# Four fast block pairs in each MLP unit, and low parts made by ScalarE and an adding DMA

## The chip, the cores and the metric

The kernel runs on one core of one Trainium2 chip. The metric is the device time of one execution in microseconds, given as the median of three runs.

## What is computed

Two layers of a decoder on one sequence of 256 rows of 2048. Each layer mixes two groups of attention heads and then runs an MLP; the part that matters here is the MLP, which is most of the arithmetic:

```python
hm = rms_norm(x, mlp_norm)
up = jnp.square(jax.nn.relu(jnp.einsum('bsd,df->bsf', hm, w_up)))      # 2048 -> 8192
return x + jnp.einsum('bsf,fd->bsd', up, w_down)                       # 8192 -> 2048
```

Everything is in float32 and every weight is read from HBM once.

## The kernel before

**Three matmuls for one.** A float32 product is made of matmuls on a shorter format. Each weight tile is split in a high part (`whi`, a rounding copy on ScalarE) and a low part (`wlo`, weight minus high part, on VectorE); activations are split alike. One block product is then three matmuls: high by high, high by low, low by high.

**Units and pairs.** The MLP of a layer is 16 units: four quarters `q` of the hidden width, each with two up units (`n2` = 0, 1) and two down units. I call them first up, second up, first down, second down, and the four together a quarter. A unit multiplies 256 rows by a 2048 x 1024 piece of the weights. It runs over eight *pairs*; a pair is two blocks of 128 contraction rows by 1024 columns, one load of 1 MB. A pair is a 2 x 2 by 2 x 2 block product. A plain pair takes eight block products, 24 matmuls of 128 x 512, in two steps of 12. A *fast* pair (`fast(i)`, pairs 1, 3 and 5) takes seven, 21 matmuls in four steps, for which VectorE first makes sums of the weight blocks in place and in the tiles `ts` (128x1024) and `t4` (`steps`, line 1208), and the activations get three extra blocks (`forms`, line 402).

**Banks and the end of a unit.** The sums of products lie in eight PSUM banks, 1 to 8. Plain steps add to banks 2 and 4, then 3 and 8; fast steps to 2 and 3, 4, 5 and 7, 1 and 6. At the end a tail on ScalarE and VectorE combines them (`down_tail`, `up_tail`): after the last fast pair a copy of bank 1, a difference with bank 6 and sums with 5 and 7; after the last plain steps one addition for each of banks 2, 4, 3 and 8. The next unit starts with banks 2 and 4, and may touch a bank only when the tail has read it. After an up unit TensorE also turns the squared result (transposes behind the first two steps of the next unit, line 1389).

**Who sets the order.** `Plan` (line 42) takes all pieces of a layer's MLP with lengths and dependences, lets TensorE and the load queue run in the order of writing, and on VectorE and ScalarE takes the ready piece that is due first. The result is a fixed order for each engine; at run time each engine works through its queue in order and stands still at a piece that isn't ready. Its lengths are

```python
        MM, TR, V2, V1, A2, A1 = 0.227, 0.108, 1.15, 0.61, 1.0, 0.55
        RING, RAWS = 5, 4
```

`RING` says that five tiles of high and five of low parts exist: a step's tile can be written when TensorE is through with the step five before. `RAWS` says the same of the loaded weights: a load waits until the pair four before has been read (`load`, line 1157; `parts`, line 1179).

**GpSimd** builds constants at the start (`build_constants`, line 238), clears a tile `kdz` in each layer and does some work in the attention; in the MLP it has nothing to do.

Of the kernel before, what the change touches and what calls it, by code (L numbers as in the profile page):

```python
# [17 lines left out]
P = 128  # L18
EPS = 1e-6
WARM0, WARM1 = 8, 6  # L20
DEPTH = 2
D = 2048
T = 256
# [16 lines left out]
class Plan:  # L40

# [26 lines left out]
    def run(self):  # L68
# [8 lines left out]
        line = {e: [p for p in self.pieces if p.engine == e] for e in ("PE", "SP")}  # L77
        free = dict.fromkeys(("PE", "SP", "DVE", "ACT"), 0.0)
# [48 lines left out]
def trunk_kernel(  # L127
# [60 lines left out]
    ATT = ("v4", "lr", "lrT", "ha", "hh", "hl", "hA", "on", "dec", "S", "kdz", "row", "bc")  # L188
    MLP = ("whi5", "wlo5", "sxh", "sx", "ts", "t4", "raw2")
# [36 lines left out]
    ident16 = cpool.tile([P, P], BF16, name="ident16")  # L226
    mask16 = cpool.tile([P, P], BF16, name="mask16")
    tri = cpool.tile([P, P], F32R, name="tri")
    nones = cpool.tile([P, P], F32R, name="nones")
    gmask = cpool.tile([P, CHUNK], F32, name="gmask")  # L230
    reset = cpool.tile([P, T], F32, name="reset")
    kdz = {}

# [4 lines left out]
    def build_constants():  # L238
        nc.vector.tensor_copy(ident16, ident)
# [8 lines left out]
        tri_f, nones_f = tmp("t2", [P, P], bufs=4), tmp("t2", [P, P], bufs=4)  # L248
# [32 lines left out]
    def load_gains(b, srcs):  # L281
        r = 0
        graw[b] = tmp("t2", [P, P], bufs=4)[: (NA, NB)[b]]
# [18 lines left out]
    wg = cpool.tile([RANK + 1, 512], F32, name="wg")  # L302

    def load_gate_up(l):
        nc.sync.dma_start(wg[0:RANK], w_gate_up[l])
        nc.sync.dma_start(wg[RANK : RANK + 1], b_gate[l : l + 1, :])
# [91 lines left out]
    def fast(i):  # L398
        return i in (1, 3, 5)

    def forms(op, i, t, tag):
# [6 lines left out]
        def sums():  # L408
            a11, a21, a12, a22 = (t[:, k, r * P : (r + 1) * P] for k in range(2) for r in range(2))
            e.append(tmp("e", [P, 3, P], bufs=2))  # L410
# [5 lines left out]
        def high():  # L416
            if e:
                op.x[i] = tmp(tag, [P, 3, 2, P], F32R, bufs=3)
                todo.append((op.x[i], e[0]))
# [10 lines left out]
    def operand_parts(op, n, h2, key, l, place):  # L430
# [30 lines left out]
        def scaled():  # L461
            t = tmp("t2", [P, 2, T], bufs=4)
# [17 lines left out]
    def norm_squares(n, ssq):  # L480
        for tt in range(NT):
            junk = tmp("t2", [P, 512], bufs=4)
# [124 lines left out]
    def join(acc):  # L607

        t = tmp("t2", [P, 2, T], bufs=4)
# [4 lines left out]
    def head_sums(ss, src, nh):  # L614

        sq = tmp("t2", [P, 512], bufs=4)
# [55 lines left out]
    def sb_scores(qT, kT, h):  # L672
# [11 lines left out]
        for j in range(2):  # L684
            for o in (zA[:, j * T : j * T + P], zB[:, j * P : (j + 1) * P]):
                nc.tensor.matmul(
                    o, ident16, mask16, start=False, stop=(j == 1), skip_group_check=True
# [16 lines left out]
    def sb_weights(za, zb, sph, spl):  # L704
        for part in (spl, sph):
            p0, p1 = part[:, : 2 * T], part[:, 2 * T :]
            upper = za.rearrange("p (h t) -> p h t", t=T)[:, :, P:T]
            for o, lhs, rhs in (
                (za, tri, p0), (zb, tri, p1),
                (upper, nones, p1.rearrange("p (h t) -> p h t", t=P)),  # L710
# [65 lines left out]
    for l in range(DEPTH):  # L776
# [290 lines left out]
        def pair_order(u):  # L1067

            if units[u][0] != "o":
                return range(8), {j for j in range(8) if fast(j)}  # L1070
# [544 lines left out]
```

## Time and profile before

| | us |
|---|---|
| median of three runs | 2185.19 (2185.18 to 2186.57) |
| the profiled execution | 2186.74 |
| its span, first to last instruction | 2185.0 |
| TensorE busy in it | 2176.2 |
| VectorE | 1850.9 |
| ScalarE | 1275.3 |
| GpSimd | 38.0 |

The span is shorter than the execution's own time by what lies around the first and the last instruction, 1.74 us. The profile's page has a table of engines, a chain of the work that ended last, and groups of instructions by line; the trace also answers with busy times by stretch and with single instructions in order of time. Matmul durations overlap there (each shows 0.39 us while the next starts 0.23 us later), so distances of starts are read, not durations.

### The profile page before, as it was taken

How to read it: one execution, taken by the hardware profiler on the slowest of the kernel's cores; microseconds unless marked ns; L12 is line 12 of the kernel's file. 1: busy time of each engine (PE TensorE's matmuls, PEld its weight loads, DVE VectorE, ACT ScalarE, POOL GpSimd, SP SyncE). 2: the span in 40 equal slices, each digit the busy share in tenths (PEclk: the TensorE clock that was granted, in tenths of full speed). 3: DMA queues.
4: the chain of work that ended last, by engine and by line, in shares of the span. 5: the costliest groups of instructions: out<-in, count | busy, mean ns of one | idle time of the engine just before them, and what ended most of it. 6: DMA issues, size and time to landing. Idle time of an engine off the chain costs nothing.

```text
span 2185.0 us, 27186 instructions
## 1 busy us (share of the span) xinstructions
PE 2176.2 (100%) x10352; PEld 1803.3 (83%) x10352; DVE 1850.9 (85%) x2386; ACT 1275.3 (58%) x1651; POOL 38.0 (2%) x64
## 2 busy tenths in 40 slices
PE   9999999999999999999999999999999999999999
PEld 7988778888888888888888887788888888888887
DVE  5677569999999999999957775799999999999998
ACT  5555356665566566466555553666665655665663
POOL 0020000000000000000000200000000000000000
PEclk9999999999999999999999999999999999999999
DMA  6654455466556556656556544555656565565564
GB/s 225 196 162 154 154 174 193 156 211 211 188 198 204 184 200 202 212 187 198 174 157 193 172 157 153 174 174 193 213 173 211 198 207 193 193 212 184 201 199 148
DMA packets 144359, 408.98 MB, mean 187 GB/s; under 512 B 6650, under 2 KB 31810, under 8 KB 144228
## 3 DMA queue, kind: packets, MB, share of 16 engines
q1 hardware_dynamic: 144228, 407.24, 56.7%
q8 instruction: 81, 1.33, 0.2%
q14 instruction: 50, 0.41, 0.1%
HBM read 405.12 MB, written 2.10 MB: 186 GB/s over the span
## 4 chain that ended last, share of the span: by engine, by line
PE 98%; DVE 1%; issue 0%; ACT 0%; DMA 0%; POOL 0%; SPq 0%; ACTq 0%
PE acc L549 6%; PE acc L551 6%; PE acc L550 6%; PE acc L596 3%; PE acc L600 1%; PE ps L1017 1%; PE ps L1029 1%; PE ps L976 0%; PE ps L712 0%; PE ps L658 0%; PE ps L676 0%; DVE wlo L1195 0%; PE ps L441 0%; PE ps L993 0%; PE ps L876 0%
## 5 line engine op out<-in xcount | busy, mean ns | idle before, releaser
L1191 ACT ACTIVATE whi<-raw 128x1024 fp32r<-128x1024 f32 x592 | 616.3, 1057 | 347.9 <-ACT whi L1191 11.5
L1195 DVE TENSOR_TENSOR wlo<-raw,whi 128x1024 fp32r<-128x1024 f32 x592 | 716.8, 1220 | 90.6 <-ACT whi L1191 85.6
L532 DVE TENSOR_TENSOR wlo<-raw,whi 128x1024 fp32r<-128x1024 f32 (+2 forms) x194 | 220.5, 1140 | 133.2 <-ACT whi L530 133.0
L530 ACT ACTIVATE whi<-raw 128x1024 fp32r<-128x1024 f32 (+2 forms) x194 | 189.7, 983 | 205.9 <-PE acc L551 156.3
L549 PE MATMUL acc<-whi,act 128*128 128x512 f32 (+2 forms) x640 | 243.1, 380 | 0.5 <-ACT act L451 0.5
L550 PE MATMUL acc<-wlo,act 128*128 128x512 f32 (+2 forms) x640 | 237.9, 372 | 0.0
L551 PE MATMUL acc<-whi,act 128*128 128x512 f32 (+2 forms) x640 | 237.5, 371 | 0.0
L1191 ACT ACTIVATE whi<-t 128x512 fp32r<-128x512 f32 x104 | 65.6, 631 | 162.8 <-DVE t L1058 154.8
L549 PEld LDWEIGHTS acc<-whi,act 128*128 128x128 f32 x640 | 121.2, 189 | 23.6 <-issue 4.1
L551 PEld LDWEIGHTS acc<-whi,act 128*128 128x128 f32 x640 | 120.9, 189 | 21.4 <-issue 0.7
L550 PEld LDWEIGHTS acc<-wlo,act 128*128 128x128 f32 x640 | 121.1, 189 | 19.1 <-issue 0.7
L1195 DVE TENSOR_TENSOR wlo<-ts,whi 128x1024 fp32r<-128x1024 f32 x104 | 127.2, 1223 | 7.3 <-ACT whi L1191 6.4
L1191 ACT ACTIVATE whi<-ts 128x1024 fp32r<-128x1024 f32 x104 | 109.6, 1054 | 35.1 <-PE m__2427_11949 L1284 2.1
L1058 DVE TENSOR_TENSOR ts<-raw 128x1024 f32<-128x1024 f32 x104 | 127.0, 1221 | 1.3
L596 PE MATMUL acc<-act,whi 128*128 128x512 f32 x256 | 91.9, 402 | 0.0
L1195 DVE TENSOR_TENSOR wlo<-t,whi 128x512 fp32r<-128x512 f32 x104 | 71.2, 685 | 2.8 <-ACT whi L1191 2.8
L600 PE MATMUL acc<-act,wlo 128*128 128x256 f32 x256 | 71.8, 280 | 0.0
L1058 DVE TENSOR_TENSOR raw<-ts,raw 128x512 f32<-128x512 f32 x104 | 71.2, 684 | 0.1
L1058 DVE TENSOR_TENSOR t<-raw 128x512 f32<-128x512 f32 x104 | 71.2, 684 | 0.1
L1368 ACT ACTIVATE act<-act,st 128x512 f32<-128x512 f32 x64 | 44.3, 717 | 26.5 <-DVE act L1058 26.5
L596 PEld LDWEIGHTS acc<-act,whi 128*128 128x128 f32 x256 | 48.1, 188 | 11.1
L600 PEld LDWEIGHTS acc<-act,wlo 128*128 128x128 f32 x256 | 48.4, 189 | 0.1
(2748 smaller groups left out, 5163.2 us busy)
## 6 DMA issues: line engine op xcount, KB each, us to landing
raw<-in_w_up_dram SPq DMA_DIRECT2D x128, 1024.0 KB, 5.1
raw<-in_w_down_dram SPq DMA_DIRECT2D x128, 1024.0 KB, 5.2
raw<-in_w_in_dram SPq DMA_DIRECT2D x84, 1024.0 KB, 5.2
raw<-in_w_o_dram SPq DMA_DIRECT2D x32, 1024.0 KB, 5.2
raw<-in_w_in_dram SPq DMA_DIRECT2D x14, 512.0 KB, 6.6
raw<-in_w_in_dram SPq DMA_DIRECT2D x8, 544.0 KB, 3.8
out_dram<-xb SPq DMA_DIRECT2D x8, 256.0 KB, 3.4
xb<-in_x_dram SPq DMA_DIRECT2D x3, 512.0 KB, 8.0
```

What stands on the lines that cost most here:

```text
L530: newest["hi"] = nc.scalar.activation(h, r, AF.Copy).ins
L532: newest["lo"] = nc.vector.tensor_tensor(lo[:, q : q + step, :width], r, f32(h), ALU.subtract).ins
L549: nc.tensor.matmul(o, xh[:, sl], whi[:, j, :width], start=first, stop=False)
L550: nc.tensor.matmul(o, xh[:, sl], wlo[:, j, :width], start=False, stop=False)
L551: st["mm"] = nc.tensor.matmul(o, xl[:, sl], whi[:, j, :width], start=False, stop=last).ins
L596: nc.tensor.matmul(acc[:, f, :], whi[:, j, sl], op.both(k), start=(k == 0), stop=False, skip_group_check=True,)
L600: nc.tensor.matmul(acc[:, f, T:], wlo[:, j, sl], xh, start=False, stop=(k == KT - 1), skip_group_check=True,)
L1017: nc.tensor.matmul(o, sc[:, (2 * tt + j) * P : (2 * tt + j + 1) * P], v[:, tt, vc + j * P : vc + (j + 1) * P], start=first, stop=False, sk ...
L1058: nc.vector.tensor_tensor(dst, a, b, op)
L1191: nc.scalar.activation(box["h"][:, :n], src(), AF.Copy)
L1195: nc.vector.tensor_tensor(box["l"][:, :n], src(), f32(box["h"][:, :n]), ALU.subtract)
L1368: nc.scalar.activation(box[h][:, tt, :], box[h][:, tt, :], AF.Relu, scale=rr[:, tt : tt + 1],)
```

## The change

In the MLP's up and down units pair 6 becomes fast as well (four of eight). Pairs 2 and 7 stay plain, but their low parts are no longer made by VectorE: ScalarE writes the negated high part into a tile `dlo` (two exist), and a DMA queued on GpSimd adds the weights to it. The steps stand in a new order, in which the steps of pairs 2 and 3 alternate, and a fast pair's steps run 2 and 3; 5 and 7; 1 and 6; 4. The low tiles of VectorE become four; the sum that went to `t4` is written in place. To make room, constants of the attention move into tiles that live only through the attention and are built again for layer 1, attention outputs `on` get two tiles for four, and the sums of the activations share the tiles `t2` (five for four).

```diff
+STEPS = [0, 0, 1, 1, 1, 1, 2, 3, 3, 2, 3, 3, 4, 4, 5, 5, 5, 5, 6, 6, 6, 6, 7, 7]
+FAST = (1, 3, 5, 6)
+ADDED = (2, 7)
...
-        RING, RAWS = 5, 4
+        RING, LOWS, ADDS, RAWS = 5, 4, 2, 4
...
+            return STEPS, FAST
+
+        def step_banks(kind, is_fast):
+
+            if kind == "g":
+                return (1, 6), (1, 6)
+            return ((2, 3), (5, 7), (1, 6), (4,)) if is_fast else ((2, 4), (3, 8))
...
+            def negated():
+                box["l"] = tmp("dlo", [P, 2, 512], F32R, bufs=ADDS)
+                nc.scalar.activation(box["l"], src(), AF.Copy, scale=-1.0)
+
+            def add_weights():
+                nc.gpsimd.dma_start(f32(box["l"]), src(), accum_op=ALU.add)
+
+            if by_dma:
+                m = add("ACT", A2, negated, deps, dlo[-ADDS] if len(dlo) >= ADDS else [])
+                lo = add("POOL", 2.7, add_weights, m, lag=7.0)
+                dlo.append([])
+                readers.extend((m, lo))
+            h = add("ACT", A2 if n == 2 else A1, high, deps, whi[-RING], last.get("h"))
+            whi.append([])
+            if not by_dma:
+                lo = add("DVE", V2 if n == 2 else V1, low, h, wlo[-LOWS], last.get("l"))
...
+                        by_dma=kind in ("up", "down") and j in ADDED,
...
-            t4 = add("DVE", V1, fourth, t2, sums4[-1] if sums4 else [])
+            t4 = vector(w(1, 0), w(0, 1), w(1, 0), t2, low[1:3])
...
+                if kind != "g" and k == max(last_use[m] for m in (5, 7, 1, 6)):
                     tails[u][0](p)
+                for c, ms in enumerate(((2, 4), (3, 8))):
+                    if kind != "g" and k == max(last_use[m] for m in ms):
+                        tails[u][1](c, p)
...
             load_gate_up(l)
+            after(2, build_constants)
```

The steps of a unit after the change are numbered 0 to 23, as `STEPS` lists them: 18 to 21 are pair 6, 22 and 23 pair 7.

VectorE's queue at the end of a first down unit (layer 0, first quarter), before the change. `xb` are the output tiles, `m1__` to `m8__` the banks, `t2` the tail's scratch; `wlo` are low parts, of the unit's last pair and then of the next unit's first pair (`raw2_934`); `ts_958` is the sum for the next unit's pair 1.

```order
L1195 TENSOR_TENSOR wlo_951_4767<-raw_926_4649,whi_946_4746 128x1024
L1058 TENSOR_TENSOR xb0_101<-m1__912_4583,xb0_101 128x512
L1058 TENSOR_TENSOR xb1_102<-t2_949_4756,xb1_102 128x512
L1195 TENSOR_TENSOR wlo_954_4787<-raw2_934_4680,whi_950_4764 128x1024
L1058 TENSOR_TENSOR t2_949_4756<-m7__908_4573,t2_949_4756 128x512
L1195 TENSOR_TENSOR wlo5_955_4796<-raw2_934_4680,whi5_953_4784 128x1024
L1058 TENSOR_TENSOR xb0_101<-xb0_101,t2_949_4756 128x512
L1058 TENSOR_TENSOR xb0_101<-m2__883_4469,xb0_101 128x512
L1058 TENSOR_TENSOR ts_958_4816<-raw_940_4716 128x1024
L1058 TENSOR_TENSOR xb0_101<-m4__886_4482,xb0_101 128x512
```

The same place after the change. The two low parts of the next unit are `wlo_966` and `wlo_969`.

```order
L1066 TENSOR_TENSOR xb0_94<-m1__916_4594,xb0_94 128x512
L1213 TENSOR_TENSOR wlo_966_4828<-raw2_943_4717,whi5_964_4819 128x1024
L1066 TENSOR_TENSOR t2_965_4826<-m6__919_4602,t2_965_4826 128x512
L1213 TENSOR_TENSOR wlo_969_4844<-raw2_943_4717,whi_967_4833 128x1024
L1066 TENSOR_TENSOR xb1_95<-t2_965_4826,xb1_95 128x512
L1066 TENSOR_TENSOR xb0_94<-m2__890_4484,xb0_94 128x512
L1066 TENSOR_TENSOR t2_965_4826<-m7__915_4589,t2_965_4826 128x512
L1066 TENSOR_TENSOR ts_971_4863<-raw_953_4767 128x1024
L1066 TENSOR_TENSOR xb0_94<-xb0_94,t2_965_4826 128x512
L1066 TENSOR_TENSOR xb1_95<-m3__898_4524,xb1_95 128x512
L1066 TENSOR_TENSOR xb0_94<-m4__893_4497,xb0_94 128x512
```

The addition that frees bank 4 now has two low parts, a sum and seven tail operations ahead of it, counted from the one that reads bank 1; between the last fast step and the next unit TensorE now has 27 matmuls where it had 48.

VectorE's queue at the end of a second up unit before the change (layer 0, first quarter; `act` holds the up unit's result, `wlo` are low parts of the next unit's first pair).

```order
L1058 TENSOR_TENSOR t2_872_4396<-m6__832_4214,act_868_4383 128x512
L1195 TENSOR_TENSOR wlo_873_4404<-raw2_851_4310,whi_871_4394 128x1024
L1058 TENSOR_TENSOR act_868_4383<-m7__826_4198,t2_872_4396 128x512
L1058 TENSOR_TENSOR act_869_4384<-m5__824_4188,t2_872_4396 128x512
L1058 TENSOR_TENSOR act_869_4384<-m5__824_4188,act_868_4383 128x512
L1195 TENSOR_TENSOR wlo_876_4425<-raw2_851_4310,whi_875_4414 128x1024
L1058 TENSOR_TENSOR ts_878_4435<-raw_859_4344 128x1024
L1058 TENSOR_TENSOR act_868_4383<-m2__800_4089,act_868_4383 128x512
```

The same place after the change.

```order
L1213 TENSOR_TENSOR wlo_882_4436<-raw2_857_4325,whi_879_4428 128x1024
L1066 TENSOR_TENSOR t2_884_4449<-m6__835_4215,act_880_4433 128x512
L1213 TENSOR_TENSOR wlo_886_4453<-raw2_857_4325,whi_883_4441 128x1024
L1066 TENSOR_TENSOR act_880_4433<-m7__830_4200,t2_884_4449 128x512
L1066 TENSOR_TENSOR act_881_4434<-m5__828_4190,t2_884_4449 128x512
L1066 TENSOR_TENSOR act_881_4434<-m5__828_4190,act_880_4433 128x512
L1066 TENSOR_TENSOR ts_888_4472<-raw_868_4377 128x1024
L1066 TENSOR_TENSOR act_880_4433<-m2__806_4097,act_880_4433 128x512
```

The order is nearly the same, with the low parts a place or two earlier against the tail; the sum for the next pair 1 stands ahead of the addition from bank 2 in both.

ScalarE's queue in the first down unit before the change: high parts of pair 5's last two steps and of the plain pairs 6 and 7.

```order
L1191 ACTIVATE whi_935_4688<-ts_923_4630 128x1024
L1191 ACTIVATE whi_938_4706<-raw_897_4528 128x1024
L1191 ACTIVATE whi5_941_4721<-raw_915_4595 128x1024
L1191 ACTIVATE whi_943_4731<-raw_915_4595 128x1024
L1191 ACTIVATE whi_944_4736<-raw_926_4649 128x1024
L1191 ACTIVATE whi_946_4746<-raw_926_4649 128x1024
```

The same place after the change: high parts of steps 16 and 17, then the two negated copies for steps 22 and 23, then the high parts of steps 18 to 20.

```order
L1209 ACTIVATE whi_942_4714<-raw_914_4587 128x1024
L1209 ACTIVATE whi_946_4736<-raw_914_4587 128x512
L1219 ACTIVATE dlo_948_4746<-raw_937_4687 128x1024
L1219 ACTIVATE dlo_949_4748<-raw_937_4687 128x1024
L1209 ACTIVATE whi_951_4759<-raw_927_4640 128x1024
L1209 ACTIVATE whi5_954_4769<-ts_950_4751 128x1024
L1209 ACTIVATE whi_956_4780<-raw_927_4640 128x1024
```

The two `dlo` copies are new there, and a copy that waits holds up the high parts behind it.

## Rows read from the trace of the kernel before

**Rows 1.** The page's span, and its table of engines: busy us, share, instructions.

```profile
span 2185.0 us, 27186 instructions
PE 2176.2 (100%) x10352; PEld 1803.3 (83%) x10352; DVE 1850.9 (85%) x2386; ACT 1275.3 (58%) x1651; POOL 38.0 (2%) x64
```

**Rows 2.** The page's chain of work that ended last, by engine.

```profile
PE 98%; DVE 1%; issue 0%; ACT 0%; DMA 0%; POOL 0%; SPq 0%; ACTq 0%
```

**Rows 3.** Busy times by stretch; one quarter of layer 0's MLP.

```profile
core 0: us, PE busy (x) PEld busy (x) DVE busy (x) ACT busy (x) POOL busy (x), PEclk, DMA share, GB/s
630.99:800.53 169.54, 169.54 (x765) 140.70 (x764) 157.55 (x188) 101.96 (x119) 0.00 (x0) 1.00 0.60 199
```

**Rows 4.** Timeline (start, us, engine, line): one matmul and its like one pairing later.

```profile
637.57 0.39 PE L1282 MATMUL m__1122_5588<-whi,act 128*128 128x512 f32 x1
...
647.77 0.39 PE L1282 MATMUL m__1122_5588<-whi,act 128*128 128x512 f32 x1
```

**Rows 5.** Timeline of VectorE in a second up unit.

```profile
635.29 0.29 DVE L411 TENSOR_TENSOR e<-act 128x128 f32<-128x128 f32 x1
635.61 0.29 DVE L412 TENSOR_TENSOR act<-act 128x128 f32<-128x128 f32 x1
...
640.52 0.55 DVE L426 TENSOR_TENSOR sx<-e,sx 128x384 fp32r<-128x384 f32 x1
...
647.81 1.22 DVE L1195 TENSOR_TENSOR wlo<-raw,whi 128x1024 fp32r<-128x1024 f32 x1
648.95 0.69 DVE L1058 TENSOR_TENSOR raw<-ts,raw 128x512 f32<-128x512 f32 x1
649.55 1.22 DVE L1195 TENSOR_TENSOR wlo<-raw,whi 128x1024 fp32r<-128x1024 f32 x1
```

**Rows 6.** Timeline of ScalarE in the same unit, a 128x512 high part.

```profile
641.17 0.62 ACT L1191 ACTIVATE whi<-t 128x512 fp32r<-128x512 f32 x1
```

**Rows 7.** Timeline at the end of layer 0's first down unit, TensorE and VectorE.

```profile
533.52 0.39 PE L1284 MATMUL m__912_4583<-whi,act 128*128 128x512 f32 x1
...
543.33 0.69 DVE L1058 TENSOR_TENSOR xb<-m__886_4482,xb 128x512 f32<-128x512 f32 x1
...
545.30 0.39 PE L1282 MATMUL m__959_4834<-whi,act 128*128 128x512 f32 x1
...
546.66 0.39 PE L1282 MATMUL m__960_4843<-whi,act 128*128 128x512 f32 x1
```

**Rows 8.** Timeline and chain: three hand-overs, TensorE to ScalarE, to VectorE, to TensorE.

```profile
642.78 0.39 PE L1284 MATMUL m__1101_5502<-whi,act 128*128 128x512 f32 x1
643.21 1.06 ACT L1191 ACTIVATE whi<-raw 128x1024 fp32r<-128x1024 f32 x1 [0.46 <-PE m__1101_5502 L1284]
...
656.18 1.06 ACT L1191 ACTIVATE whi<-raw 128x1024 fp32r<-128x1024 f32 x1 [1.65 <-PE m__1111_5540 L1284]
657.27 1.23 DVE L1195 TENSOR_TENSOR wlo<-raw,whi 128x1024 fp32r<-128x1024 f32 x1 [1.48 <-ACT whi L1191]
...
437.69 0.04 issue
437.74 0.50 PE m__715_3698 L1283
```

**Rows 9.** DMA issues: queue, count, KB each, median us to landing.

```profile
raw<-in_w_up_dram SPq DMA_DIRECT2D x128, 1024.0 KB, 5.1
out_dram<-xb SPq DMA_DIRECT2D x8, 256.0 KB, 3.4
```

**Rows 10.** Timeline of GpSimd and VectorE in layer 0's attention.

```profile
131.67 6.10 POOL L910 TENSOR_TENSOR act<-act,row 128x512 f32<-128x512 f32 x3
...
132.59 1.79 DVE L532 TENSOR_TENSOR wlo<-raw,whi 128x1024 fp32r<-128x1024 f32 x1 [0.45 <-ACT whi L530]
...
137.68 1.23 DVE L532 TENSOR_TENSOR wlo<-raw,whi 128x1024 fp32r<-128x1024 f32 x1 [1.07 <-ACT whi L530]
```

**Rows 11.** Groups of GpSimd's instructions by line: count, busy, mean ns.

```profile
L236 POOL MEMSET kdz<- 128x1536 f32 x2 | 2.8, 1382 | 811.9 <-DVE wlo L1195 811.9
```

More of the change, by code (lines that the diff above doesn't have):

```diff
@@ L246, in build_constants @@
         )
-        tri_f, nones_f = tmp("t2", [P, P], bufs=4), tmp("t2", [P, P], bufs=4)
+        tri_f, nones_f = (tmp("t2", [P, 512], bufs=T2)[:, :P] for _ in range(2))
         nc.gpsimd.memset(tri_f, -1.0)
@@ L1084, in trunk_kernel @@
             whi.append([p])
-            wlo.append([p])
+        wlo.extend([p] for p in before[-LOWS:])
         gate_done = {}
@@ new lines, in trunk_kernel @@
+            of_pair, uses = {j: 0 for j in order}, []
+            for j in order:
+                uses.append(step_banks(kind, j in quick)[of_pair[j]])
+                of_pair[j] += 1
+            last_use = {m: k for k, ms in enumerate(uses) for m in ms}
+            begun, p, running = set(), {}, {}
+            was = units[u - 1] if u else None
+            for k, j in enumerate(order):
+                if j not in running:
+                    running[j] = steps(u, j, j in quick, *load(u, j))
+                (box, h, lo, users), prods = next(running[j])
+                ready = done.get((kind, q, j))
+                for m, blocks in prods:
+                    begin, end = m not in begun, last_use[m] == k
+                    begun.add(m)
+                    p[m] = add(
+                        "PE", 3 * MM * len(blocks),
+                        lambda a=(m, blocks, box, begin, end): product(*a),
+                        h, lo, ready, free[m] if begin else [],
+                    )
+                    for tile_users in users:
+                        tile_users.append(p[m])
+                if kind == "g" and k == 4 or kind == "o" and n2 == 0 and k == 5:
+                    turn_gated()
+                    turn_gated()
+                if k < 2 and was and was[0] == "up":
+                    tails[u - 1][2](k)
+                if k < 2 and was and was[0] == "o":
+                    n = 2 * was[2] + k
+                    for h2 in range(2):
+                        done["up", 0, 2 * n + h2] = turned(
+                            n, h2, ((5, 7), (1, 6))[k][h2], hm, "mlp", l, sums=True
+                        )
+                if u + 1 == len(units) and k < 2 and l + 1 < DEPTH:
+                    for h2 in range(2):
+                        turned(k, h2, ((5, 7), (1, 6))[k][h2], hT, "attn", l + 1)
+                if kind != "g" and k == max(last_use[m] for m in (5, 7, 1, 6)):
```

193 lines of the change are left out of this document (77 added, 116 removed).

## The prediction

> **What bounds the kernel now.** First the page's table of engines: TensorE is busy 2176.2 of the 2185.0 us span [rows 1]. Then the chain that ended last: 98% of it is TensorE [rows 2]. So the end moves only if TensorE gets less to do, or is made to wait. The table of stretches, cut at one point of the repeating quarter of the MLP (two up units, two down units), gives 169.54 us a quarter, with VectorE busy 157.55, ScalarE 101.96, the DMA engines a 0.60 share [rows 3]. VectorE has 12 us to spare, so it is the next bound. Slots come from the timeline: 45 matmuls lie between the two rows of [rows 4], so one takes (647.77 - 637.57)/45 = 0.2267 us. On VectorE the distance of starts counts, not the duration shown: a 128x1024 operation holds the engine 1.14 us and shows 1.22, a 128x512 one 0.60 and shows 0.69 [rows 5].
>
> **What is removed.** One more pair by seven products saves three matmuls a unit, 32 units: 96 x 0.2267 = 21.8 us, all on the path, since TensorE waits nowhere in a quarter.
>
> **VectorE's total.** Per quarter the low parts of pairs 2 and 7 (16 of 128x1024) leave: -16 x 1.14 = -18.2. Pair 6 keeps its two low parts and gains, over four units, 4 x (2 of 128x1024 and 3 of 128x512): 4 x (2 x 1.14 + 3 x 0.60) = +16.3. Its operand's sums and third part add 4 x 0.32 + 0.55 = +1.8 [rows 5]. Net about 0 (-0.1): 157.5 us of work in a quarter that shrinks to 169.54 - 12 x 0.2267 = 166.8. In total it fits, with 9 us to spare. ScalarE gets 16 negated copies and pair 6's extra parts, at most 16 x 1.06 + 4 x (1.06 + 0.62) + 0.6 = 24 us [rows 6, 8], and stands at 126 of 166.8: no bound.
>
> **The end of a unit is where it pinches.** Before, two plain pairs followed the last fast one, so after step (1, 6) TensorE had 48 matmuls, 10.9 us, before it touched the banks again. In a first down unit it ended that step at 533.75, started the next unit at 545.30 and asked for bank 4 at 546.66, and VectorE's add had read that bank by 543.33 + 0.69 = 544.02: 2.6 us early [rows 7]. Now step 20 is followed by 3 + 24 = 27 matmuls, 6.12 us. Count from the end of step 20's slots. A matmul's result can be used 0.20 us after its slot ends (642.78 + 0.23 to 643.21), VectorE starts 0.03 after ScalarE ends, TensorE 0.04 after VectorE ends [rows 8]. I lay VectorE's new order, as the change's section shows it, end to end.
> First down to second down: the add from bank 1 can start at -0.48 and is through at 0.12; next unit's low part of step 0, 1.26; difference from bank 6, 1.86; low part of step 1, 3.00; add, 3.60; bank 2, 4.20; bank 7, 4.80; the next pair's 128x1024 sum, which stands ahead of three of the adds, 5.94; two adds, 7.14; bank 4 starts at 7.14 and frees it at 7.14 + 0.69 + 0.04 = 7.87. TensorE asks for bank 2 at 6.12 (there) and for bank 4 six matmuls on, at 7.48: it waits 0.39. The second down unit has the same order before a next up unit: 0.39.
> Second up to first down: low part of step 0 ends at 1.07 (ScalarE's half of it comes at -0.10), difference 1.67, low part 2.81, three adds 4.61, the sum 5.75, then bank 2, free at 6.48 against 6.12: 0.36. First up to second up: the sum comes ahead of all this, the difference starts at 0.41, bank 2 is free at 5.82: no wait.
> Waits: 8 x 0.39 + 6 x 0.39 + 8 x 0.36 = 8.3 us (the last down unit of a layer has other work behind it). Bounds: 0, if VectorE gets in one small operation earlier; and if it comes one 128x1024 operation late everywhere, 22 x 1.14 + 8 x 0.84 = 32 us more. I take 8.3, the sum by the order itself.
>
> **The adding transfers.** 128 of 512 KB, four a unit, queued on GpSimd, which has nothing else there. The trace of before has none. The tighter place is pair 7: its first negated copy stands behind step 17's small copy on ScalarE, which waits for the end of step 12; it ends 0.20 + 0.62 + 1.06 = 1.9 us after that [rows 6, 8], and step 22 begins 54 matmuls, 12.25 us, after it. So 10.4 us are left for the add, from queue to landing. Pair 2's copy waits for step 22's bank of the unit before, ends at 4.7 on the count above, and is asked for at 6.12 + 0.39 + 45 x 0.2267 = 16.7: 12.0 us. Nearest rows: a 256 KB store lands in 3.4 us, a 1 MB load in 5.1 [rows 9], and an add reads half a megabyte twice. A GpSimd operation takes 2.0 [rows 10]. From below 3.4, from above two loads and one such operation, 12.4. I take 5.1 + 2.0 = 7.1, since the load moves what the add reads: hidden, cost 0. The raw tiles of these pairs are held about 8 us longer; the load that wants such a tile is used four pairs on, 20 us, which hides it. The DMA share goes from 0.60 to 0.76 (8 MB more on 32) or 0.91 (each read twice).
>
> **At nothing.** The constants built again for layer 1: GpSimd's 1.38 us clearing [rows 11] and some fills stand ahead of three small casts on VectorE, behind which the next low parts queue; the first unit's four finished halves (4 x 12 x 0.2267 = 10.9 us of TensorE) cover it; uncovered it is some 3 us, once. Four low tiles in place of five: in pairs 5 and 6 a tile comes free 15 matmuls (3.4 us) before its step and its making takes 1.3 to 2.5; uncovered, one low part, 1.14 us, a unit. Smaller buffers of attention outputs: the tiles live three half-groups; nothing.
>
> **Sum.** 2186.74 for the profiled execution (1.74 outside its span), -21.8 + 8.3 = -13.5: 2173.2. The median of the three runs lies 1.55 under it: 2171.7.
>
> **Rivals.** *All hidden:* VectorE's idle time before a unit's end takes up the 0.4 us, and the whole 21.8 comes: 2163.4. For it: the waits are a tenth of a tail each. Against it: an in-order queue does not reorder.
> *The adds land late (the slower side):* each microsecond past 10.4 is paid in all 32 units at step 22. At 10.8 it has eaten the gain (13.5/32 = 0.42); at the upper bound, 12.4, it is 2.0 x 32 = 64 us: 2236. For it: four reads of 512 KB share 16 engines with loads. Against it: a 1 MB load needs half of it.
> *GpSimd slows VectorE:* the trace has a place for it. Beside GpSimd's 128x512 operations VectorE's low parts take 1.79 us, and 1.23 right after [rows 10]. If issuing an add stretches one low part by 0.56, a quarter loses 16 x 0.56 = 9.0, just what VectorE has left; if it stretches two, 18, so 9 x 8 = 72 us too much: 2244. It decides from one low part an add. In the Trainium skill, "SBUF — State Buffer", section "Who interferes with whom", a VectorE instruction with two SBUF inputs contends with a GpSimd instruction that reads SBUF; the trace agrees for computing instructions (1.79 against 1.23), and no run here shows it for the making of a DMA. By that rule the time would be the forecast's 2172 if making the descriptors reads no SBUF, and this rival's 2244 if it does.
> *The transfers fill up:* at a 0.91 share everything on the queues takes longer. If loads take 8.0 us for 5.1, an add takes 2.9 more too, 10.0, and a copy that comes 0.9 late for its tile leaves TensorE waiting 0.5 us a unit: 2171.7 + 16 = 2188. For it: pairs 2 and 7 hold raw tiles longest just when the adds run. Against it: the share is a mean, and 0.76 if the add's own reading counts for nothing.
>
> **Chances.** Forecast (2167 to 2178) 0.42; all hidden 0.22; adds late 0.15; VectorE slowed 0.11; transfers fill 0.10. The range 2163 to 2187 holds the first two, half of the last two and little of the third, 0.78. A measurement of this kernel can tell 0.2%, 4.4 us, from no change. Faster: 0.42 + 0.22 + 0.06 = 0.70; within: 0.11; slower: 0.19.
>
> **What would show it.** Right: 96 matmuls fewer, a quarter of 167 to 168 us, TensorE waiting some 0.4 us for VectorE at the first or second bank of down units and of units after down units and nowhere else, adds that land in 6 to 9 us. Wrong: waits of TensorE on a DMA of the negated tile; low parts of 1.5 us and more; a VectorE without idle time; waits inside a unit.

## The result, and the profile after

The changed kernel takes 2189.48 us (median of 21 runs, 2186.86 to 2190.90), the kernel before 2185.57 (21 runs). The ratio is 1.0017, with a 95% interval of 1.0010 to 1.0024: slower by a sixth of a per cent, where the forecast was 2171.7 and the range ended at 2187.

| | before | after |
|---|---|---|
| the profiled execution / its span | 2186.74 / 2185.0 us | 2189.26 / 2187.5 us |
| matmuls | 10352 | 10256 |
| a quarter of the MLP, as in [rows 3] | 169.54 us | 169.51 us |

The page of the changed kernel: the table of engines, and the chain of work that ended last, by engine.

```profile
PE 2162.9 (99%) x10256; PEld 1781.3 (81%) x10256; DVE 1852.4 (85%) x2469; ACT 1451.4 (66%) x1855; POOL 196.1 (9%) x202
...
PE 67%; DMA 14%; DVE 11%; issue 5%; ACT 1%; POOL 1%; SPq 0%; DVEq 0%; POOLq 0%; ACTq 0%
```

The 96 matmuls are gone. But the chain, 98% TensorE before [rows 2], now runs through DMA and VectorE for a quarter of the span. Busy times of the same quarter as in [rows 3], cut at the same point of the program (two others take 169.84 and 170.10 us):

```profile
core 0: us, PE busy (x) PEld busy (x) DVE busy (x) ACT busy (x) POOL busy (x), PEclk, DMA share, GB/s
629.66:799.17 169.51, 168.29 (x754) 137.98 (x753) 157.51 (x198) 123.65 (x146) 19.30 (x17) 1.00 0.88 248
```

VectorE has the work that was forecast (157.51 of 157.5), ScalarE too (124 of at most 126). What is new is the DMA share, 0.88 for 0.60. The page's DMA queues (packets, MB, share of 16 engines) and issues (count, KB each, median us to landing):

```profile
q1 hardware_dynamic: 144228, 407.24, 55.5%
q0 software_dynamic: 34816, 67.12, 18.1%
...
raw<-in_w_up_dram SPq DMA_DIRECT2D x128, 1024.0 KB, 5.1
raw<-in_w_down_dram SPq DMA_DIRECT2D x128, 1024.0 KB, 6.6
...
dlo<-raw POOLq DMA_DIRECT2D x128, 512.0 KB, 8.8
```

Queue q0 holds the adds. One add holds all 16 engines for 0.181 x 2187.5/128 = 3.1 us. The loads hold them for 0.555 x 2187.5/407.24 = 2.98 us a MB, so 3.1 us for one of 1024 KB (1.05 MB). An add of half a megabyte costs the engines as much as a load of a whole one, and it lands in 8.8 us at the median, not 7.1.

**Where TensorE waits: at the second half of pair 7.** A piece of the chain in layer 0's third quarter (start, us, what):

```profile
866.89 0.92 POOL dlo L1222
867.82 13.55 DMA dlo<-raw
881.41 0.50 PE m__1514_7421 L1313
```

Both adds of pair 7 are issued 0.95 us apart, and share the engines with each other and with the loads. The second takes 13.55 us, and step 23 waits 1.33 us for it. The median of all adds hides this: over the 32 units pair 7's first add lands in 5.8 us at the median and in 6.0 at most, the second in 12.1 (6.65 to 13.55). Such waits, counted as spacing of matmuls beyond a slot, come to some 9 us in the run, 10.8 with the slow restarts behind them.

**And from first up to second up unit, where none was forecast.** A piece of the chain (start, us, what), then the timeline of VectorE and TensorE there, layer 0, third quarter (start, us, engine, line, operation, and in brackets idle time and who ended it):

```profile
781.31 8.41 DMA raw<-in_w_up_dram
```

```profile
789.81 1.23 DVE L1066 TENSOR_TENSOR ts<-raw 128x1024 f32<-128x1024 f32 x1 [3.04 <-DMA raw<-in_w_up_dram]
790.95 0.68 DVE L1066 TENSOR_TENSOR t<-m__1370_6736,act 128x512 f32<-128x512 f32 x1
...
795.62 0.68 DVE L1066 TENSOR_TENSOR act<-m__1352_6661,act 128x512 f32<-128x512 f32 x1
...
796.44 0.47 PE L1312 MATMUL m__1423_6996<-whi,act 128*128 128x512 f32 x1 [0.78 <-DVE act L1066]
```

The sum `ts` for the next unit's pair 1 stands in VectorE's queue ahead of the whole tail. Its weights come late, VectorE stands still for 3.04 us, and the tail, which frees bank 2 at 796.3, is late with it. All eight such turns wait, 8.6 us together. The load in question was queued at 781.31 and took 8.4 us to land; the eight take 7.7 to 9.7 us, beside the second add of pair 7. They are not queued late: 26.6 to 28.4 us after the start of the unit before, in the run without adds (e1, below) 27.1 to 28.4. Other loads, of pair 3 above all, do start some 5 us later than there, because the next load into a raw tile has to wait for an add that still reads it, but TensorE has no wait behind those. Waits of VectorE and of the load queue (us in total, times, longest):

```profile
DVE ts L1066 <- DMA raw<-in_w_up_dram: 22.9, 8, 3.5
...
SPq L1188 <- DMA dlo<-raw: 218.8, 60, 7.0
```

The second line says who ended the queue's waits and not that they grew: this line's waits are 1477.5 us in all here and 1460.0 without adds.

**And at the turn to layer 1.** ScalarE there waits 2.40 us for a load of the attention's weights, which takes 8.9 us to land (5.0 in e1), and 2.64 us for the next; low parts behind them stand in VectorE's queue ahead of the last tail, and TensorE waits for the output tiles. That next load in the chain, then the timeline:

```profile
1087.54 8.27 DMA raw<-in_w_in_dram
```

```profile
1092.14 1.23 DVE L540 TENSOR_TENSOR wlo<-raw,whi 128x1024 fp32r<-128x1024 f32 x1 [2.65 <-ACT whi L538]
...
1101.09 0.33 PE L449 MATMUL ps<-ident,xb 128*128 128x128 f32 x1 [1.75 <-DVE xb L1066]
```

### The profile page after: what moved, and what is told of

Same layout as the page of the kernel before. It is cut to its first block, busy times and chain, and to the rows that moved or that the text cites. A ratio compares the mean times of both kernels' runs of the same rounds, so it can differ in the third digit from the quotient of the medians.

```text
span 2187.5 us, 28276 instructions
## 1 busy us (share of the span) xinstructions
PE 2162.9 (99%) x10256; PEld 1781.3 (81%) x10256; DVE 1852.4 (85%) x2469; ACT 1451.4 (66%) x1855; POOL 196.1 (9%) x202
## 3 DMA queue, kind: packets, MB, share of 16 engines
q1 hardware_dynamic: 144228, 407.24, 55.5%
q0 software_dynamic: 34816, 67.12, 18.1%
## 4 chain that ended last, share of the span: by engine, by line
PE 67%; DMA 14%; DVE 11%; issue 5%; ACT 1%; POOL 1%; SPq 0%; DVEq 0%; POOLq 0%; ACTq 0%
DMA dlo<-raw 7%; PE acc L557 6%; PE acc L558 6%; PE acc L559 6%; DVE wlo L1213 5%; DMA raw<-in_w_up_dram 4%; PE acc L604 3%; DMA raw<-in_w_down_dram 2%; PE acc L608 1%; DVE ts L1066 1%; DVE act L1066 1%; DVE raw L1066 1%; DVE xb L1066 1%; ACT whi L1209 1%; POOL dlo L1222 1%
## 5 line engine op out<-in xcount | busy, mean ns | idle before, releaser
L1209 ACT ACTIVATE whi<-raw 128x1024 fp32r<-128x1024 f32 (+1 forms) x728 | 701.5, 976 | 296.2 <-DVE raw L1066 45.2
L1213 DVE TENSOR_TENSOR wlo<-raw,whi 128x1024 fp32r<-128x1024 f32 (+1 forms) x600 | 654.6, 1097 | 65.8 <-ACT whi L1209 53.9
L1222 POOL DMA_DIRECT2D dlo<-raw x128 | 154.7, 1267 | 1502.4 <-ACT dlo L1219 1211.1
L1066 DVE TENSOR_TENSOR ts<-raw 128x1024 f32<-128x1024 f32 x136 | 165.6, 1218 | 24.6 <-DMA raw<-in_w_up_dram 22.9
L1209 ACT ACTIVATE whi<-ts 128x1024 fp32r<-128x1024 f32 x136 | 144.1, 1060 | 44.8 <-DVE ts L1066 10.7
L1219 ACT ACTIVATE dlo<-raw 128x1024 fp32r<-128x1024 f32 x128 | 130.8, 1048 | 59.0 <-DMA raw<-in_w_down_dram 35.5
L1213 DVE TENSOR_TENSOR wlo<-ts,whi 128x1024 fp32r<-128x1024 f32 x136 | 165.6, 1218 | 1.6 <-PE m__2482_12170 L1313 0.8
L1066 DVE TENSOR_TENSOR raw<-raw 128x512 f32<-128x512 f32 x136 | 93.6, 688 | 2.9
L1066 DVE TENSOR_TENSOR raw<-ts,raw 128x512 f32<-128x512 f32 x136 | 92.7, 682 | 0.0
L1398 ACT ACTIVATE act<-act,st 128x512 f32<-128x512 f32 x64 | 41.7, 711 | 13.4 <-DVE act L1066 13.3
```

The costliest lines, as they stand in the source:

```text
L1066: nc.vector.tensor_tensor(dst, a, b, op)
L1209: nc.scalar.activation(box["h"][:, :n], src(), AF.Copy)
L1213: nc.vector.tensor_tensor(box["l"][:, :n], src(), f32(box["h"][:, :n]), ALU.subtract)
L1219: nc.scalar.activation(box["l"], src(), AF.Copy, scale=-1.0)
L1222: nc.gpsimd.dma_start(f32(box["l"]), src(), accum_op=ALU.add)
```

## The experiments

The theory after the result: the adds fill the DMA engines, so that they and the loads land late, and the order of the queues passes this on to TensorE. The rivals: the shorter end of a unit does it by itself; the number of DMAs or GpSimd does it; only VectorE's order does it. A ratio is to the kernel before, timed beside it, with its 95% interval. Each expectation gives two readings. Six runs fit neither: e1, e4, e8 and g2 came between the two, e6 and e13 above both.

| run | us | ratio |
|---|---|---|
| e1: no adds | 2173.80 | 0.9946 (0.9931 to 0.9961) |
| e2: adds of half the bytes | 2173.43 | 0.9946 (0.9931 to 0.9961) |
| e3: copies for adds | 2173.92 | 0.9948 (0.9933 to 0.9963) |
| e4: tail before the sum | 2182.18 | 0.9982 (0.9972 to 0.9992) |
| e6: that, and adds due earlier | 2196.70 | 1.0044 (1.0027 to 1.0061) |
| e8: adds of 4 KB pieces | 2183.84 | 0.9990 (0.9981 to 0.9999) |
| v_24: adds at pairs 2 and 4 | 2349.96 | 1.0752 (1.0730 to 1.0773) |
| v_04: adds at pairs 0 and 4 | 2230.94 | 1.0204 (1.0189 to 1.0219) |
| v_lay: 4 KB pieces, loads by halves | 2183.94 | 0.9990 (0.9981 to 0.9999) |
| v_lay_tail: that and e4 | 2182.47 | 0.9979 (0.9970 to 0.9988) |
| e13: no adds, and e4 | 2177.23 | 0.9959 (0.9944 to 0.9974) |
| e7: adds alone | 2199.53 | 1.0061 (1.0047 to 1.0074) |
| g3: no adds, planner mended | 2165.85 | 0.9909 (0.9896 to 0.9923) |
| g2: the change, planner mended | 2178.90 | 0.9973 (0.9962 to 0.9984) |
| g1: v_lay, planner mended | 2173.06 | 0.9944 (0.9931 to 0.9956) |
| e12: pair 6 fast alone | 2241.22 | 1.0254 (1.0235 to 1.0273) |
| h1: kernel before, planner mended | 2182.86 | 0.9987 (0.9977 to 0.9997) |

### What the adds cost: e1, e2, e3

```diff
 def add_weights():
-    nc.gpsimd.dma_start(f32(box["l"]), src(), accum_op=ALU.add)
+    pass                                                                  # e1
+    nc.gpsimd.dma_start(f32(box["l"][:, :1]), src()[:, :1], accum_op=ALU.add)  # e2
+    nc.gpsimd.dma_start(f32(box["l"]), src())                             # e3
```

> The adding DMA is left out (the low parts of pairs 2 and 7 are then only the negated copy, so the sum is not completed); everything else, the order of every other queue too, is the changed kernel's 2189.5 us. If the adds take the time through the DMA engines (theory), the waits at the second half of pair 7 go (9.2 us in the trace of the changed kernel), the loads of weights land in 5.1 us again, the waits from a first to a second up unit go with them (8.6 us), and some 2.5 us at the first two banks of other units stay: 2165 to 2172 us. If instead the shorter end of a unit makes the waits by itself (rival), the up units keep 1.07 us a turn and only the waits on the added tile go: 2178 to 2181 us. If GpSimd's issuing were the cause it would also go, but then the low parts of VectorE would become shorter than 1218 ns.

> Each adding DMA adds only the first of its tile's two blocks, 256 KB for 512 (the other is left out of the sum); as many DMAs, as many GpSimd instructions. If bytes on the DMA engines are the price: adds land in 4 to 6 us, the DMA share of the MLP falls from 0.86 to about 0.73, the second half of pair 7 is in time, and most of the turn of the up units goes: 2168 to 2176 us. If the price is per DMA (issue on GpSimd, fixed cost): nearly the changed kernel, 2185 to 2190 us.

> The same DMA from the same tile to the same tile, but it copies and does not add (the low part is then the weight itself). If adding costs engine time beyond moving the 512 KB (in the trace an add's packet of 2 KB takes about twice the time per byte of a load's): DMA share near 0.73, copies land in 5 to 6 us, 2168 to 2178 us. If a copy inside SBUF costs the same as an add: share 0.86, landing 8.8 us, 2187 to 2190 us.

All three came to 2173.4 to 2173.9. So the adds cost 2189.5 - 2173.8 = 15.7 us, and the number of DMAs is not the price: e2 and e3 have as many. Queue q0 and the landing, first of e2, then of e3:

```profile
q0 software_dynamic: 18432, 33.56, 9.1%
...
dlo<-raw POOLq DMA_DIRECT2D x128, 256.0 KB, 5.0
```

```profile
q0 software_dynamic: 18432, 67.12, 8.2%
...
dlo<-raw POOLq DMA_DIRECT2D x128, 512.0 KB, 4.9
```

A copy of the same bytes holds the engines for 8.2% of the span, an add for 18.1%. In the Trainium skill, "Collectives: The Full Stack", section "The bandwidth ceiling: the fold count and why AG ≠ RS ≠ AR", a ReduceScatter, whose DMAs add, runs at half the rate of an AllGather, whose DMAs copy, because an add reads two sources and not because of the adding itself, with a measured ratio of 1.93. This case's trace shows a like ratio for a DMA inside SBUF, 18.1/8.2 = 2.2; no run here parts the second read from the adding.

In e1 TensorE's waits in the MLP stand where the forecast put them and nowhere else, with their sizes; e1's own expectation had left only 2.5 us of them, and so lay too low. Waits of TensorE in e1 (us in total, times, longest), one of 8 and one of 14 like it:

```profile
PE m__1199_5910 L1312 <- DVE act L1066: 0.3, 1, 0.3
...
PE m__1046_5208 L1312 <- DVE xb L1066: 0.2, 1, 0.2
```

And VectorE's sum `ts` no longer waits for its load (group of the page: count, busy, mean ns, idle before):

```profile
L1066 DVE TENSOR_TENSOR ts<-raw 128x1024 f32<-128x1024 f32 x136 | 165.6, 1217 | 0.8
```

By the spacing of matmuls TensorE's waits are 8 x 0.45 us at bank 2 from second up to first down (forecast 8 x 0.36), 8 x 0.38 at bank 4 from first to second down (8 x 0.39), 6 x 0.39 at bank 4 from second down to first up (6 x 0.39), and none from first up to second up. A matmul after a wait also starts some 0.08 us slower than a slot, which the forecast left out.

### The order of VectorE as a patch: e4, e13, e6

```diff
-t13 = add("DVE", V2, first, ld, sums13[-1] if sums13 else [])
+tail = [free[m] for m in (2, 4)] if j == 1 and kind in ("up", "down") else []
+t13 = add("DVE", V2, first, ld, sums13[-1] if sums13 else [], *tail)
```

> The adds stay; only the order on VectorE is changed: the 128x1024 sum for the next unit's pair 1 comes behind the additions that free banks 2 and 4. If the late load does harm only because this sum stands ahead of the tail in VectorE's queue (theory), the waits from first to second up unit (8.6 us) and most of those at the first banks of other units (2.6 us) go with their restarts: 2176 to 2180 us, with the 9.2 us at pair 7 left. If the load itself is what matters (rival), the wait moves to the second step of pair 1 and the time stays at 2187 to 2190 us.

> No adds (left out of the sum) and the tail first: what the order of VectorE alone is worth. In the run without adds 9.0 us of waits at the first banks of units and some 3 us of restarts were left at 2173.8 us. Theory (these waits are the order's): 2163 to 2168 us, near the 2163.4 at which all of the 96 matmuls would be gained. Rival (VectorE is short of time at a unit's end in any order): 2172 to 2175 us.

With adds the edit gains 7.3 us: the waits from first to second up fall from 8.6 to 2.7 (e4's trace is of its longest execution, 2186.55). Without adds it loses 3.4. The rival of e13 fell too, as g3 shows below; in its trace VectorE puts a low part where the sum was, and six first-to-second-up turns now wait as well: 14 waits of 0.3 us on an addition to `act`, where e1 has 8. So the patch only changes which long operation slips into the tail.

e6 adds to this that the planner thinks the adds due 7 us earlier:

```diff
-p.due = ... - p.length - p.lag - self.GAP
+p.due = ... - p.length - p.lag - self.GAP - 7.0 * (p.engine == 'POOL')
```

> The tail comes before the next unit's sum on VectorE, as in the run of that edit alone (2182.2 us), and in the planner the adds are due 7 us earlier, so that ScalarE makes the negated copies sooner where the weights are there. If the waits at the second half of pair 7 come from the place of the copies in ScalarE's queue: they go, 2172 to 2176 us. If they come from weights of pair 7 that land late and from the adds' 8 to 13 us on busy engines: the copies can't start sooner, and the time stays at 2180 to 2184 us.

It is slower than either reading had it. In the second down units the copies of pair 7 come 1.7 us sooner before their step than in the changed kernel, and the waits on pair 7's added tile there are gone; in the first down and second up units, where the other such waits are, they come no sooner (13.7 and 13.5 us before it, for 13.5 and 13.7). Late weights don't hold them there: the copies that wait for weights, below, are pair 2's, all but one. What is lost is elsewhere: TensorE waits 16 times some 0.4 us for a bank that a square on ScalarE (L1427) has to read first. Wait of ScalarE's copies in e6 (in the changed kernel 35.5 us, 12 times; in e4 50.8, 17 times):

```profile
ACT dlo L1219 <- DMA raw<-in_w_down_dram: 45.8, 15, 4.3
```

### Other pairs for the adds: v_24, v_04

```diff
-ADDED = (2, 7)
+ADDED = (2, 4)     # v_24; (0, 4) in v_04; both with the edit of e4
```

> Tail first, and pairs 2 and 4 take the adds in place of 2 and 7 (VectorE makes the low parts of pair 7). Theory (the adds are the same load for the DMA engines, but no step waits for one at a unit's end): the 9 us at pair 7 go unless the second halves of pair 4 come late in their turn; VectorE gets its low parts of pair 7 into the end of a unit: 2172 to 2182 us. Rival (any add on engines that are 86% busy lands too late): 2185 us or more.

> Tail first, and pairs 0 and 4 take the adds: the adds of pair 0 fall in the end of the unit before, where VectorE is short of time, so its queue there gets two low parts (2.3 us) shorter and two of pair 7 longer. Theory: the adds are spread apart by four pairs, each alone on the engines with the loads, so each lands in about 6 us instead of 8.8: 2170 to 2178 us. Rival: the loads of a unit's start and pair 0's adds collide, 2185 us or more.

Both theories were wrong; the rivals' "2185 us or more" held. Waits of TensorE, the longest in v_24 (one of 34 on `dlo`, 103.6 us together), then the two longest in v_04 (27 on `dlo`, 25.0 us, and 13 on low parts of VectorE, 14.5):

```profile
PE m__2909_14265 L1313 <- DMA dlo<-raw: 4.9, 1, 4.9
```

```profile
PE m__3132_15326 L1313 <- DMA dlo<-raw: 2.4, 1, 2.4
PE m__1350_6667 L1313 <- DVE wlo L1213: 2.3, 1, 2.3
```

Pair 4's first step comes three after pair 2's last, and there are two `dlo` tiles, so its copies wait until TensorE is through with pair 2's; ScalarE in v_24:

```profile
711.72 1.07 ACT L1219 ACTIVATE dlo<-raw 128x1024 fp32r<-128x1024 f32 x1 [0.46 <-PE m__1201_5949 L1313]
```

Some 40 us of v_24's loss come on top of the waits, which are up to 4.9 us long. Behind them the granted clock of TensorE stands at 0.5, its level of 1.2 GHz, in 25 stretches of 113 us together, and over 200 matmuls there follow each other at 0.43 us in place of 0.23. The mean granted clock is 0.976; the changed kernel's is 1.0.

The change's choice of pairs 2 and 7 was the best of the three. In v_04 the pairs with adds have more steps between them, yet the second add of pair 0 lands in 12.6 us at the median; why was not looked into.

### Pieces of 4 KB: e8, v_lay, v_lay_tail

```diff
+if units[u][0] in ("up", "down") and i in ADDED:
+    for c in range(2):
+        nc.sync.dma_start(
+            dst[:, c, :].rearrange("p (k n) -> p k n", k=2),
+            weights(u, i)[:, :, c * 512 : (c + 1) * 512],
+        )
+else:
+    nc.sync.dma_start(dst, weights(u, i))
...
-nc.gpsimd.dma_start(f32(box["l"]), src(), accum_op=ALU.add)
+nc.gpsimd.dma_start(
+    f32(box["l"]).rearrange("p k n -> p (k n)"),
+    src().rearrange("p k n -> p (k n)"), accum_op=ALU.add,
+)
```

This is v_lay, where the copies and high parts read the halves too; e8 has only the second part, with `r()[:, c, :]` as the add's source, so its adds take other weights than the product asks for.

> The adds read one whole row of 4 KB in each partition of the loaded tile instead of two pieces of 2 KB (so other weights are added, and the sum is not the right one); all else is the changed kernel's, 512 KB an add. In the changed kernel the adds took 34816 packets on their queue and 18.1% of the engines, plain copies of the same bytes 18432 packets and 8.2%. If the price comes from packets of 2 KB: 18432 packets, some 10%, 2172 to 2177 us. If adding itself doubles the engines' time: 34816 packets or not, 16 to 18%, landing near 8.8 us, 2185 to 2190 us.

> The changed kernel with the weights of pairs 2 and 7 loaded by two DMAs of 512 KB, column half by column half, so that each add reads 4 KB in a row in each partition (and the right weights, unlike the run with whole rows). All queues of the computing engines keep their order. If it is the adds' time to land that is paid (theory): adds in about 6.2 us, no waits at the second half of pair 7, 4 us left at the first to second up turns: 2182 to 2185 us. If loads in pieces of 2 KB cost the DMA engines as much as the adds save (rival): 2187 to 2192 us.

> The same loads and adds, and the tail before the next unit's sum on VectorE. Theory: the two causes add up, so the 4 us at the up turns and most of the 9 us that VectorE's order leaves at the other ends of units go too: 2170 to 2177 us, 0.5% under the kernel before. Rival (a late load moves the wait elsewhere whatever the order): 2182 to 2186 us.

Queue and landing in e8:

```profile
q0 software_dynamic: 18432, 67.12, 17.2%
...
dlo<-raw POOLq DMA_DIRECT2D x128, 512.0 KB, 6.2
```

The packets halve, and the engines' time hardly falls (17.2% for 18.1): it is that the DMA adds, and not its packets, that costs them, as the second reading of e8's expectation had it. GpSimd's issuing is not the price either: an issue takes 862 ns in e2 and in e8, and e2 pays nothing, e8 10 us. Yet the adds land in 6.2 us for 8.8, the waits at the second half of pair 7 go, and 5.6 us are gained, which that reading did not foresee; it is not more, because e1's 9.0 us at the ends of units are back. v_lay does the same with each add's own weights (7.3 us to landing, 2183.9). v_lay_tail has the 9 us at the ends of units still, as e13 would have it.

### The halves of the change: e7, e12

```diff
-STEPS = [0, 0, 1, 1, 1, 1, 2, 3, 3, 2, 3, 3, 4, 4, 5, 5, 5, 5, 6, 6, 6, 6, 7, 7]
-FAST = (1, 3, 5, 6)
+STEPS = [0, 0, 1, 1, 1, 1, 2, 3, 3, 2, 3, 3, 4, 4, 5, 5, 5, 5, 6, 6, 7, 7]    # e7
+FAST = (1, 3, 5)                                                               # e7
...
-ADDED = (2, 7)
+ADDED = ()                                                                     # e12
```

> Pair 6 is plain again (22 steps a unit, VectorE makes its low parts), the adds for pairs 2 and 7 stay: the second half of the change alone. 96 matmuls more than the changed kernel, VectorE with 18 us less to do in a quarter than before the change, 48 matmuls behind the last fast step again. If the adds hurt only through a unit's short end: 2185 to 2188 us, as before the change. If they hurt by landing late and by late loads whatever the end is: 2190 to 2205 us.

> The other half of the change alone: pair 6 fast, no adds, VectorE makes all low parts again (18.2 us more in a quarter, by the working of the prediction 175.7 us of work in a quarter of 166.8). If VectorE is then the bound: 8 x 9 = 72 us or more over the forecast, 2235 to 2260 us. If it has hidden reserves: 2170 to 2200 us.

The adds alone make the kernel before 13.3 us slower, with 48 matmuls behind the last fast step: their price doesn't hang on the short end. The longest wait on an add in e7, of 15 (10.6 us):

```profile
PE m__3304_16517 L1313 <- DMA dlo<-raw: 1.3, 1, 1.3
```

Pair 6 alone is bound by VectorE, which is busy for 177.94 of 180.00 us in the MLP of e12:

```profile
600.00:780.00 180.00, 174.36 (x769) 140.31 (x768) 177.94 (x216) 111.11 (x132) 0.00 (x0) 1.00 0.55 187
```

### The order mended at its source: g3, g2, g1, h1

`Plan.run` handles one event at a time, and fills an engine as soon as it is free. When a piece on VectorE ends, its follower on VectorE is announced by a second event of the same instant, so that another ready piece, one of 128x1024 say, can go first at each link of the tail.

```diff
+            if events and events[0][0] <= now + 1e-9:
+                continue
             for e in free:
                 if free[e] > now + 1e-9:
                     continue
```

> No adds (left out of the sum). The planner is changed in one place: it takes all pieces that come ready at one instant before it fills an engine. Without that, a piece whose only hindrance is the piece that just ended on VectorE counts as not ready, so that another piece, a 128x1024 one, slips into each tail. Theory (the 9.0 us of waits at first banks and their restarts are this order's): 2163 to 2167 us, near the 2163.4 of all 96 matmuls gained. Rival (VectorE has no time for it in any order): 2171 to 2175 us, as with the old order (2173.8).

> The changed kernel with that order of the planner, adds and loads as they were (pieces of 2 KB). If late adds and late loads set the waits in any order (theory): 5 to 9 us come off, 2180 to 2185 us, with waits on the added tile left at the second half of pair 7. If the order was all of it: 2172 to 2176 us.

> That order and the adds of 4 KB pieces (loads of pairs 2 and 7 by column halves). Adds land in 6.2 us and no step waits for them; the order takes the 9 us at the ends of units away. Theory: 2168 to 2176 us. Rival (the late loads move the waits on, as with the tail-first edit): 2180 to 2184 us.

> The kernel before, with only the planner's order changed as in the three kernels of that edit. If the waits of 0.4 us come from the change's short end (theory): the kernel before has only some 2.5 us of gaps in its MLP stretches, so 2181 to 2185 us. If the order was a cost of its own in both kernels (rival): 2175 to 2179 us, 8 us less as without adds.

The same quarter of the MLP without adds, in e1 (old order) and in g3 (mended):

```profile
627.79:796.26 168.47, 167.74 (x754) 138.22 (x753) 157.59 (x197) 123.90 (x145) 0.00 (x0) 1.00 0.58 200
```

```profile
626.04:793.48 167.44, 167.44 (x754) 138.36 (x753) 158.29 (x197) 123.42 (x145) 0.00 (x0) 1.00 0.59 201
```

167.44 us, all of it TensorE's. So 2173.8 - 2165.85 = 8.0 us were the order's, and VectorE had the time. In this order adds of 2 KB pieces cost 2178.9 - 2165.85 = 13.0 us, of 4 KB pieces 7.2. Neither trace has a wait of TensorE on an add left, against g2's theory: what is paid there is not an add's own landing. In g2 VectorE's sums `ts` wait 33.4 us for loads (in g3 for none), and 5.7 us of the 13.0 lie in the turn to layer 1. h1 shows that the mended order is worth only 2.9 us to the kernel before, so it is the short end that makes the order matter.

g1 beats both kernels: 2173.06 us, 0.56% under the kernel before. Its quarter, at a DMA share of 0.87, loses next to nothing:

```profile
627.04:794.56 167.52, 167.41 (x754) 138.36 (x753) 158.08 (x197) 123.69 (x146) 14.23 (x17) 1.00 0.87 251
```

Of its 7.2 us over g3 some 4.6 lie in the turn to layer 1, most of it where VectorE's queue still has a low part ahead of the tail, waiting for late weights, in g1 too:

```profile
1085.33 2.36 DVE L542 TENSOR_TENSOR wlo<-raw,whi 128x1024 fp32r<-128x1024 f32 x2 [2.74 <-ACT whi L540]
...
1092.74 0.33 PE L451 MATMUL ps<-ident,xb 128*128 128x128 f32 x1 [1.36 <-DVE xb L1068]
```

That place was left as it is.

## Why the prediction was wrong, point by point

- **The 96 matmuls**: right. 10256 are left, and with the adds left out and next to nothing in the way (g3) the time is 2165.85; the all-hidden figure was 2163.4.
- **VectorE's and ScalarE's totals**: right, 157.51 us in a quarter for 157.5, 123.65 for at most 126.
- **The end of a unit, 8.3 us**: right in size and place where there are no adds: 3.6 + 3.1 + 2.3 = 9.0 us in e1, and no wait from first to second up. With the changed kernel's adds the sum is 2.6 us at these three places, because TensorE has already lost time inside the units: unit by unit, what it loses at pair 7 and what it then waits at the next first bank add up to some 0.4 us or are more at pair 7 alone. Laying out a queue by hand from distances of starts held to 0.1 us a wait. That this order was VectorE's only choice ("an in-order queue does not reorder") was true of the queue, not of the planner (g3).
- **The adds, taken at 7.1 us and priced at 0**: this is the step that failed. They cost 15.7 us. Three things were missed. First, the second add of pair 7. The budget was checked for that pair's first copy only, as "the tighter place", and there it held: 10.3 us from issue to step 22, landing in 5.8 at the median. But the two adds are issued 0.95 us apart and share the engines, so the second lands in 12.1 at the median and 13.55 at most; the product that wants it comes 12.1 us after its issue (e8, where nothing waits there), and TensorE waits at step 23, not 22. Secondly, the estimate took an add for a load and asked only when it lands; it left out what the add takes from the loads beside it: 3.1 us of all 16 engines, as much as a load of a megabyte. The loads for `ts` beside pair 7's second add take 7.7 to 9.7 us. Thirdly, the layout of VectorE's queue from first up to second up took the weights of `ts` as there; late, they hold up the whole tail, where the forecast had no wait at all. The raw tile's longer hold, put down as hidden by "20 us", was hidden: loads start later by it, but not those behind TensorE's waits.
- **The turn to layer 1**: priced at 0 ("has other work behind it"). From the first product of layer 0's last unit to the first of the planned part of layer 1 the changed kernel takes 338.43 us, e1 335.63, the kernel before 336.36. The 2.8 us come from two loads that take 8.9 and 8.3 us to land (5.0 and 5.4 in e1), through the same kind of queue; the load that waits for an add there, 5.9 us, is the one behind them. Rebuilding the constants costs nothing that shows: e1 does it too.
- **The rivals.** *The transfers fill up*, 2188 us, is the mechanism that happened, and it had a tenth of the chance. Its inputs were nearly right: adds 10.0 us forecast, 8.8 measured; loads 8 us forecast, 7.7 to 9.7 for the loads of the `ts` that came late (but 5.1 and 6.6 at the median, and 5.0 and 6.3 without adds); share 0.91, measured 0.88. That its time lies within 2 us of the measured one is partly luck: it priced 0.5 us a unit for a late copy, and the runs have waits at step 23, from first to second up and at the turn, while most of the 8.3 us of the forecast, on which it was built, drop out. The argument against it, "the share is a mean, and 0.76 if the add's own reading counts for nothing", was the wrong one to believe. *The adds land late* at step 22 fell: they do so at step 23 and cost 9 us, not 64. *GpSimd slows VectorE* fell: low parts take 1218 ns beside the adds, 1.22 us before [rows 5]. In the quarter of above, by form:

```profile
L1213 DVE TENSOR_TENSOR wlo<-raw,whi 128x1024 fp32r<-128x1024 f32 x49 | 59.7, 1218 | 6.0 <-ACT whi L1209 5.9
```

  The rule of the Trainium skill that the prediction weighed there ("SBUF — State Buffer", section "Who interferes with whom") thus does not reach to the making of these DMAs: the trace shows none of the 0.56 us a low part that computing on GpSimd cost [rows 10].
- **The sum**: -21.8 + 9.0 and some 2 us of slow restarts, + 15.7 for the adds, is about +5; measured are +3.9.

By place the traces of the changed kernel and of e1 divide the 15.7 us so: 10.8 at the second half of pair 7 (late adds), 9.2 from first to second up and 2.8 at the turn to layer 1 (late loads), less 7.4 of e1's own waits, which TensorE no longer meets; that makes 15.4. What stays open is what each would cost without the other: in e7 nearly all of the price lies at pair 7, in g2 none. That the landing falls from 8.8 to 6.2 us with the pieces' size, while the engines' time hardly does, is shown; why was not looked into.

## What to carry to other kernels

Price a DMA twice: by when it lands, and by the time that it takes from all 16 engines; an adding DMA here took as much of them as a load of twice its bytes, and of two issued together the second took 12.1 us to land where the first took 5.8. Ask for the last transfer of a group, not for the first or the median. Where a change lifts the share of the DMA engines as here (0.60 to 0.88), look up what stands at the head of each in-order queue when a load is late: a piece that waits there holds up all that is ready behind it, and that is where a transfer that is hidden on paper is paid. And when a planner writes the order, see whether it could have chosen better before taking the waits of its order for the engine's limit.

## What the runs showed of the hardware

- An SBUF-to-SBUF add of 512 KB takes 2.2 times the engines' time of a copy of the same bytes (18.1% against 8.2% of 16 engines for 67.12 MB), and 2.1 times in pieces of 4 KB, with as many packets as the copy (17.2%).
- Pieces of 4 KB for 2 KB halve the packets and bring the landing of an add from 8.8 to 6.2 us. Issuing one on GpSimd takes 862 ns at the mean for 1267, a plain copy 724:

```profile
L1222 POOL DMA_DIRECT2D dlo<-raw x128 | 110.3, 862 | 1536.6 <-ACT dlo L1219 1238.1
```

  (the group of GpSimd's adds on the page of e8).
- At a DMA share of 0.71 to 0.73 in the MLP (e2, e3) the transfers cost TensorE nothing that the runs can tell; at 0.82 (e8) they cost 10 us, at 0.86 in the old order 15.7 us (the changed kernel). The share alone is not the price: in the mended order 0.86 cost 13.0 us (g2) and 0.85 to 0.86 cost 7.2 (g1).
